# The second product of the attention logits, over 64 rows or over 128

## The chip, the cores and the metric

The kernel runs on one core of one Trainium2 chip. The metric is the device time of one execution in microseconds: 953.86 us, the median of three runs (953.65 to 954.18), before the change. Engine names in the profile: PE is the matrix engine (TensorE), PEld its weight loads, DVE the vector engine, ACT the scalar engine, POOL the GpSimd engine, SP the engine that issues most transfers.

## The reference, cut to what matters

One layer of a decoder trunk for 512 positions of width 1024: a norm and a modulation, one wide input projection, an mLSTM branch, a differential attention branch, gates and an output projection. The change touches the logits of the attention branch only. It has eight heads; each head has two maps of queries and keys of width 64, and the same bias for both:

```
logits = jnp.einsum('bhmqd,bhmkd->bhmqk', qh[:, :, :, q0:end], kh[:, :, :, :end])
p = jax.nn.softmax(logits + bias[None, :, None], axis=-1)
a = p[:, :, 0] - lam * p[:, :, 1]
```

`q0:end` is a block of 128 queries; its keys are all positions up to `end`, so a block has 128, 256, 384 or 512 keys.

## The kernel before, in words

**Arithmetic.** Matmuls read a 32-bit type that keeps fewer bits than float32. Every operand is therefore kept as a high part and a low part (what the high part left over), and a product is made of three matmuls: high by high, low by high, high by low (`mm3`, L135 to L137).

**Logits before.** A map is only 64 wide, and an operand tile has 128 partitions. `evac_qa` writes q of map 0 as a tile with the high part in partitions 0 to 63 (`LO`) and the low part in 64 to 127 (`HI`); for map 1 the halves are exchanged. `evac_ka` writes the high part of k of a map into both halves of a tile (`kh`), so that one matmul over all 128 rows (L441) gives high by high plus low by high. The third product, high q by low k, is a matmul of its own (L442). It takes only the 64 rows in which q has its high part: `q[m][a, qs]` with `kl[a, 0:wn]`. The low parts of k of both maps lie in one tile `kl`, map 0 in its lower half, map 1 in its upper half. For each head, four query blocks and two maps make eight such pairs of matmuls, with 256, 256, 384 and 512 columns in the four blocks (`wn`), so 64 pairs in all: 32 of 256 columns, 16 of 384, 16 of 512. The result of a pair lies in one of the four PSUM buffers tagged `core`, is read by DVE (L444, bias and row minimum) and then goes through an exponential on ACT (L446).

**Around it.** The attention heads are generators (`attn_head`) that are advanced by `tick()` between the projections (`proj_b`, `proj_v`), whose weights stream in as granules of 512 KB, are split by ACT (`whi`, L100) and DVE (`wlo`, L118), and are multiplied with the resident `h_hi` and `h_lo`. So short pieces of attention stand between long runs of projection matmuls. `inorder` fixes the order of the attention matmuls among themselves; otherwise each engine executes its instructions in the order in which a scheduler has put them when the program was built. The heads work from about 66 to 340 us. After the logits a head is transposed (L471, into `core` buffers), split into the tile `sw` (L100, L118), multiplied with v (L135 to L137 with `sw` and `v`) and normalised.

**Buffers.** Tiles of one tag share a ring of buffers; a tile's first write waits until the tile that had the buffer before has been read for the last time. `qk` has ten buffers: five for each head (two q, two `kh`, one `kl`), so two heads. The tag also serves the mLSTM's q and k and, at the end, `yh`. POOL has little to do: the masks of the bias tiles (L224), a zeroed strip in each `sw` (L464), and one-off fills (L509, L564).

Of the kernel before, what the change touches and what calls it, by code (L numbers as in the profile page):

```python
# [9 lines left out]
F32 = mybir.dt.float32  # L10
F32R = mybir.dt.float32r
AF = mybir.ActivationFunctionType
ALU = mybir.AluOpType

S = 512
D = 1024
P = 128
# [48 lines left out]
def hybrid_block_kernel(ctx: ExitStack, tc: tile.TileContext, xT, x, c, wada2, wada, win, wif, wpm, wpa, wout,  # L66
                        small, lamv, bif, relb, onehot, fing, out):
    nc = tc.nc
# [3 lines left out]
    sb = ctx.enter_context(tc.tile_pool(name="sb", bufs=1))  # L72
# [6 lines left out]
    def nm(s):  # L79
        _n[0] += 1  # L80
        return f"{s}_{_n[0]}"

    def tmp(w=512, dt=F32):
        return sb.tile([P, w], dt, tag="tmp", bufs=TB, name=nm("tmp"))

    def acc_ps():
        return acc.tile([P, 512], F32, tag="acc", name=nm("acc"))

    def core_ps():
        return core.tile([P, 512], F32, tag="core", name=nm("core"))  # L90

    def out_ps():
        return core.tile([P, 512], F32, tag="core", name=nm("core"))
# [32 lines left out]
    def inorder(inst):  # L126
        if last[0] is not None:
            tc.add_manual_dep(inst.ins, last[0].ins.name,
                              mybir.DependencyInfo(mybir.DependencyClass.NoSync, mybir.DependencyReason.DATA),
                              reason="issue order")  # L130
        last[0] = inst
# [40 lines left out]
    for k in range(NK):  # L172
        t = sb.tile([P, S], F32, tag="hp", bufs=16, name=nm("xt"))
# [10 lines left out]
    make_identity(nc, ident)  # L184
    onesf = const.tile([P, P], F32, name="onesf")
    nc.vector.memset(onesf, 1.0)
    ones_w = sb.tile([P, S], F32R, tag="qk", bufs=10, name="ones_w")
    nc.vector.memset(ones_w.bitcast(F32), 1.0)
    ones_r = const.tile([P, P], F32R, name="ones_r")
    nc.vector.tensor_copy(ones_r, onesf)  # L190
# [26 lines left out]
    def bias_tile(hd):  # L217
        if hd + 2 < AH:
            toe(hd + 2)
        bt = sb.tile([P, S], F32, tag="bt", bufs=3, name=nm("bt"))  # L220
        flat = toe_d[hd].rearrange("p l -> (p l)")
        v = flat[P - 1:P - 1 + P * (RL - 1)].rearrange("(p l) -> p l", l=RL - 1)[:, 0:S]
        nc.sync.dma_start(bt, v)
        a = nc.gpsimd.affine_select(bt[:, 384:512], bt[:, 384:512], [[-1, P]], ALU.is_ge, BIG, base=0,  # L224
                                    channel_multiplier=1)
        issue_after(a, x_done[0])
        return bt
# [17 lines left out]
    for i in range(2):  # L245
        ps = core_ps()
        a = nc.tensor.matmul(ps, onesf[0:1, :], crow[:, i * S:(i + 1) * S], start=True, stop=True)
# [19 lines left out]
    for k in range(NK):  # L267
        i, start = (0, k == 0) if k < 5 else (1, k == 5)
        sq = xsum[i] if start else tmp()
        a = nc.scalar.activation(sq, xt[k], AF.Square, scale=1.0 / 32)  # L270
# [36 lines left out]
    ps = core_ps()  # L307
# [21 lines left out]
    for (a, b) in ((0, 512), (512, RL)):  # L329
        ps = core_ps()  # L330
        m = nc.tensor.matmul(ps[0:AH, 0:b - a], relt, oneh[:, a:b], start=True, stop=True)  # L331
# [44 lines left out]
        return v  # L376

    def qk_tile():
        return sb.tile([P, S], F32R, tag="qk", bufs=10, name=nm("qk"))

    def silu2(ps):
        t = tmp()
# [8 lines left out]
    LO, HI = slice(0, 64), slice(64, 128)  # L391
# [9 lines left out]
        return q  # L401


    def evac_ka(ps):
        kh, kl = [], qk_tile()
        for a, b in ((LO, HI), (HI, LO)):
            t = qk_tile()
            nc.scalar.copy(t[a], ps[a])
            nc.scalar.copy(t[b], ps[a])
            nc.vector.tensor_tensor(kl[a], ps[a], t[a].bitcast(F32), ALU.subtract)  # L410
            kh.append(t)
        return kh, kl

    ha = [None] * AH
# [9 lines left out]
    def attn_head(hd, q, k):  # L424
        while live["p"] == PB:
            yield
        live["p"] += 1
        bt = bias_tile(hd)
        vs = slice((hd % 2) * P, (hd % 2) * P + P)
        pt = sb.tile([P, 2, 1280], F32, tag="p", bufs=PB, name=nm("pt"))  # L430
        mn = sb.tile([P, NT, 2], F32, tag="mn", bufs=3, name=nm("mn"))
        ls = sb.tile([P, NT, 2], F32, tag="ls", bufs=3, name=nm("ls"))
        kh, kl = k
        yield
        for qb in range(NT):
            w = P * (qb + 1)
            wn = max(w, 256)
            qs = slice(qb * P, qb * P + P)
            for m, a in enumerate((LO, HI)):
                ps = core_ps()[:, 0:wn]  # L440
                inorder(nc.tensor.matmul(ps, q[m][:, qs], kh[m][:, 0:wn], start=True, stop=False))  # L441
                inorder(nc.tensor.matmul(ps, q[m][a, qs], kl[a, 0:wn], start=False, stop=True))  # L442
                pp = pt[:, m, QOFF[qb]:QOFF[qb] + w]
                nc.vector.tensor_tensor_reduce(pp, ps[:, 0:w], bt[:, S - w:S], 1.0, BIG, ALU.add, ALU.min,  # L444
                                               mn[:, qb, m:m + 1])
                nc.scalar.activation(pp, pp, AF.Exp, scale=-1.0, bias=mn[:, qb, m:m + 1],  # L446
                                     accum_out=ls[:, qb, m:m + 1])
            if qb > 0:
                yield
        nc.vector.reciprocal(ls, ls)  # L450
        nc.vector.tensor_scalar(ls[:, :, 1], ls[:, :, 1], nlam, None, ALU.mult)
        for qb in range(NT):
            w = P * (qb + 1)
            p1 = pt[:, 0, QOFF[qb]:QOFF[qb] + w]
            p2 = pt[:, 1, QOFF[qb]:QOFF[qb] + w]
            nc.scalar.activation(p2, p2, AF.Copy, scale=ls[:, qb, 1:2])
            nc.vector.scalar_tensor_tensor(p1, p1, ls[:, qb, 0:1], p2, ALU.mult, ALU.add)
        yield
        while live["sw"]:
            yield  # L460
        live["sw"] = 1
        sw = sb.tile([P, 2, 1408], F32R, tag="sw", name=nm("sw"))
        ah, al = sw[:, 0, :], sw[:, 1, :]
        nc.gpsimd.memset(sw[:, :, 896:1024].bitcast(F32), 0.0)  # L464
        for kbs, o0 in (((0,), KOFF[0]), ((1,), KOFF[1]), ((3, 2), KOFF[3] + P)):
            ps = core_ps()
            n = 0
            for kb in kbs:
                for qb in range(kb, NT):
                    o = QOFF[qb] + kb * P  # L470
                    inorder(nc.tensor.transpose(ps[:, n:n + P], pt[:, 0, o:o + P], ident))  # L471
                    n += P
            split(ah[:, o0:o0 + n], al[:, o0:o0 + n], ps[:, 0:n])
        live["p"] -= 1
        yield
        ps = out_ps()
        for kb in range(NT):
            c0 = min(kb, 2) * P
            a = slice(KOFF[kb], KOFF[kb] + S - c0)
            mm3(ps[:, c0:S], (va[hd][0][:, kb, vs], va[hd][1][:, kb, vs]), (ah[:, a], al[:, a]),  # L480
                kb == 0, kb == NT - 1, head=True)
        live["sw"] = 0
        o_t = sb.tile([P, S], F32, tag="z", bufs=8, name=nm("o"))
        nc.scalar.copy(o_t, ps)
        sq = tmp()
        nc.scalar.activation(sq, ps, AF.Square)
        sh, sl = tmp(dt=F32R), tmp(dt=F32R)
        split(sh, sl, sq, eng="dve")
        yield
        ps = out_ps()  # L490
        inorder(nc.tensor.matmul(ps, ones_r, sh, start=True, stop=False))
        inorder(nc.tensor.matmul(ps, ones_r, sl, start=False, stop=True))  # L492
        r = rstd(ps, 1.0 / 128)
        nc.vector.tensor_mul(o_t, o_t, r)
        while za[hd] is None:
            yield
        z = za[hd]
        nc.vector.scalar_tensor_tensor(z, o_t, agc[:, hd:hd + 1], z, ALU.mult, ALU.mult)
        ha[hd] = hp_tiles()
        split(ha[hd][0], ha[hd][1], z, eng="dve")  # L500
# [83 lines left out]
    for k in range(NK):  # L584
# [5 lines left out]
        a = nc.scalar.copy(hi, raw)  # L590
        issue_after(a, recent["act"])
        recent["act"] = a
        t, b = xt[k], mod[:, k:k + 1]
# [32 lines left out]
        if k == 4:  # L626
# [9 lines left out]
            a = nc.vector.tensor_scalar(agc, sm[:, SM_AG:SM_AG + 8], -0.5 / 256 * (1.0 - LAM_INIT), None, ALU.mult)  # L636
            mgc = const.tile([P, 16], F32, name="mgc")
            issue_after(a, h_dve)
            a = nc.vector.tensor_scalar(mgc, sm[:, SM_MG:SM_MG + 16], -0.25 / 4096, None, ALU.mult)
# [31 lines left out]
    for p in range(1, 4):  # L671
        for i in range(2):
            hd = 2 * p + i
            q = evac_qa(proj_b(C_QA + 128 * hd))
# [18 lines left out]
    ps = core_ps()  # L693
# [178 lines left out]
    for h in range(MH):  # L872
        q, k, v, hv = [], [], [], []
# [28 lines left out]
        for d in range(4):  # L902
            ps = proj_b(C_OM + 512 * h + 128 * d)
            while len(hv) <= d:
                tick()
            t = tmp()
# [4 lines left out]
            else:  # L911
                t = tmp()
# [14 lines left out]
    for b in range(4, 8):  # L927
        ps = proj_b(C_GM + 128 * b, tick if b > 4 else None)
# [11 lines left out]
    def merge(b, ps):  # L940
        nc.vector.scalar_tensor_tensor(gt[b], gt[b], 1.0, ps, ALU.add, ALU.mult)
        nc.vector.tensor_add(gt[b], gt[b], ym[b])
        t = (sb.tile([P, S], F32R, tag="qk", bufs=10, name=nm("yh")),
             sb.tile([P, S], F32R, tag="hp", bufs=16, name=nm("yl")))
        split(t[0], t[1], gt[b], eng="act")
        yt.append(t)
# [26 lines left out]
    for t in range(NT):  # L973
# [5 lines left out]
        for n, ns in enumerate(parts):  # L979
            ps = first[n] if t == 0 else acc_ps() if n % 2 == 0 else core_ps()  # L980
            ps = ps[:, 0:ns.stop - ns.start]
# [83 lines left out]
```

## Time and profile before

| what | value |
|---|---|
| median of three runs | 953.86 us (953.65 to 954.18) |
| profiled execution, its own time | 953.58 us |
| its span in the trace | 951.6 us |
| what lies outside the span | 1.98 us |
| PE busy | 937.9 us (99%), 4735 matmuls |
| DVE busy | 603.7 us (63%) |
| ACT busy | 457.3 us (48%) |
| POOL busy | 17.1 us (2%) |

A row of the timeline gives the start, the duration, the engine, the source line, the operation, the tile written and those read, the shapes, and in brackets the idle time of the engine before it with what ended it. A matmul's end is modelled, and matmuls overlap: their durations say little, and what one costs is the distance from its start to the start of the next. For PE a shape such as `64*128 64x256` is 64 rows by 128 columns of weights, and 64 rows by 256 columns that move through them.

### The profile page before, as it was taken

The page shows a single profiled execution, that of the slowest core. Times are in us where ns is not written, and L with a number is a line of the kernel's source. Part 1 is how long each engine was busy: PE and PEld are TensorE (multiplying, and loading weights), DVE is VectorE, ACT ScalarE, POOL GpSimd, SP SyncE. Part 2 cuts the span into 40 slices and gives each one's busy share as a digit, 9 for nine tenths or more (in the row PEclk, how much of TensorE's full clock was granted, in tenths as well). Part 3 has the DMA queues.
Part 4 walks back from the last instruction along what each step waited for, and adds up shares of the span by engine and source line. Part 5 has one row for each costly group of instructions (what it writes and reads, how often), then busy time and mean ns, then how long its engine had stood idle before and what let it go on. Part 6 is the DMA issues. An engine that isn't in the chain of part 4 may idle for free.

```text
span 951.6 us, 12250 instructions
## 1 busy us (share of the span) xinstructions
PE 937.9 (99%) x4735; PEld 785.3 (83%) x4735; DVE 603.7 (63%) x975; ACT 457.3 (48%) x741; POOL 17.1 (2%) x40
## 2 busy tenths in 40 slices
PE   7999999999999999999999999999999999999997
PEld 3887877887788789888889888898888998888886
DVE  7966777866755637534658545486554776747954
ACT  7455777756556745312436433363223653226432
POOL 0000000000001000000000000000000000000000
PEclk8999999999999999999999999999999999999999
DMA  9872313433322253343222222222231224335421
GB/s 342 318 207 88 101 67 108 147 133 123 127 72 90 85 181 111 118 147 111 89 90 89 89 89 89 89 90 91 87 111 67 89 101 147 129 127 193 166 67 67
DMA packets 40659, 114.95 MB, mean 121 GB/s; under 512 B 8289, under 2 KB 8553, under 8 KB 39578
## 3 DMA queue, kind: packets, MB, share of 16 engines
q1 hardware_dynamic: 40010, 113.11, 34.3%
q10 hardware_dynamic: 592, 1.07, 0.3%
q8 instruction: 37, 0.61, 0.3%
q14 instruction: 20, 0.16, 0.1%
HBM read 106.78 MB, written 10.00 MB: 123 GB/s over the span
## 4 chain that ended last, share of the span: by engine, by line
PE 97%; DMA 1%; ACT 1%; DVE 1%; SPq 0%; issue 0%; ACTq 0%
PE acc L135 27%; PE acc L136 26%; PE acc L137 26%; PE core L135 4%; PE core L136 4%; PE core L137 4%; PE core L442 2%; PE core L441 2%; PE core L471 1%; DMA relt<-in_relb_dram 1%; PE core L238 1%; DMA xt<-in_xT_dram 1%; DVE wlo L118 0%; ACT whi L100 0%; PE core L331 0%; PE core L492 0%
## 5 line engine op out<-in xcount | busy, mean ns | idle before, releaser
L135 PE MATMUL acc<-h_hi,whi 128*128 128x512 f32 x688 | 271.0, 394 | 0.4 <-DVE qk L410 0.4
L118 DVE TENSOR_TENSOR wlo<-raw,whi 128x1024 fp32r<-128x1024 f32 x129 | 157.8, 1223 | 171.7 <-ACT whi L100 168.0
L100 ACT CAST whi<-raw 128x1024 fp32r<-128x1024 f32 x129 | 135.5, 1050 | 271.4 <-PE acc L136 217.4
L136 PE MATMUL acc<-h_lo,whi 128*128 128x512 f32 x656 | 256.5, 391 | 0.0
L137 PE MATMUL acc<-h_hi,wlo 128*128 128x512 f32 x656 | 255.7, 390 | 0.0
L135 PEld LDWEIGHTS acc<-h_hi,whi 128*128 128x128 f32 x688 | 129.4, 188 | 29.3 <-issue 1.5
L137 PEld LDWEIGHTS acc<-h_hi,wlo 128*128 128x128 f32 x656 | 123.2, 188 | 26.2
L136 PEld LDWEIGHTS acc<-h_lo,whi 128*128 128x128 f32 x656 | 123.3, 188 | 24.0 <-issue 0.4
L135 PE MATMUL acc<-whi,h_hi 128*128 128x256 f32 x352 | 100.1, 284 | 0.0
L137 PE MATMUL acc<-whi,h_lo 128*128 128x256 f32 x352 | 99.6, 283 | 0.0
L136 PE MATMUL acc<-wlo,h_hi 128*128 128x256 f32 x352 | 99.6, 283 | 0.0
L135 PE MATMUL acc<-hh,whi 128*128 128x512 f32 x192 | 74.8, 389 | 0.0
L136 PE MATMUL acc<-hl,whi 128*128 128x512 f32 x192 | 74.8, 389 | 0.0
L137 PE MATMUL acc<-hh,wlo 128*128 128x512 f32 x192 | 74.7, 389 | 0.0
L135 PEld LDWEIGHTS acc<-whi,h_hi 128*128 128x128 f32 x352 | 67.4, 191 | 1.7 <-issue 0.8
L136 PEld LDWEIGHTS acc<-wlo,h_hi 128*128 128x128 f32 x352 | 67.4, 192 | 0.6
L137 PEld LDWEIGHTS acc<-whi,h_lo 128*128 128x128 f32 x352 | 67.4, 192 | 0.0
L444 DVE CUSTOM_DVE_ANT_0 pt<-core,bt 128x128 f32<-128x128 f32 (+3 forms) x64 | 30.3, 487 | 29.7 <-PE core L442 29.5
L446 ACT ACTIVATE pt<-pt,mn 128x128 f32<-128x128 f32 (+3 forms) x64 | 35.6, 558 | 19.7 <-DVE mn L444 19.2
L137 PEld LDWEIGHTS acc<-hh,wlo 128*128 128x128 f32 x192 | 36.0, 188 | 7.5
L135 PEld LDWEIGHTS acc<-hh,whi 128*128 128x128 f32 x192 | 36.1, 188 | 7.3
L136 PEld LDWEIGHTS acc<-hl,whi 128*128 128x128 f32 x192 | 36.1, 188 | 7.2
(276 smaller groups left out, 1363.5 us busy)
## 6 DMA issues: line engine op xcount, KB each, us to landing
raw<-in_win_dram SPq DMA_DIRECT2D x112, 512.0 KB, 3.3
wa<-in_wada_dram SPq DMA_DIRECT2D x8, 1024.0 KB, 7.4
raw<-in_wpm_dram SPq DMA_DIRECT2D x16, 512.0 KB, 3.3
raw<-in_wada_dram SPq DMA_DIRECT2D x8, 512.0 KB, 3.4
raw<-in_wpa_dram SPq DMA_DIRECT2D x8, 512.0 KB, 3.3
raw<-in_wout_dram SPq DMA_DIRECT2D x8, 512.0 KB, 3.3
gt_d<-tmp SPq DMA_DIRECT2D x12, 256.0 KB, 2.2
toe_d<-rev_d SPq DMA_DIRECT2D x8, 320.0 KB, 7.0
```

What stands on the lines that cost most here:

```text
L100: recent["act"] = nc.scalar.copy(dst, src)
L118: recent["dve"] = nc.vector.tensor_tensor(lo, src, hi.bitcast(F32), ALU.subtract)
L135: a = nc.tensor.matmul(ps, lhs[0], rhs[0], start=start, stop=False)
L136: b = nc.tensor.matmul(ps, lhs[l[0]], rhs[l[1]], start=False, stop=False)
L137: c = nc.tensor.matmul(ps, lhs[r[0]], rhs[r[1]], start=False, stop=stop)
L238: a = nc.tensor.matmul(idle, ones_r, ones_w, start=True, stop=True)
L441: inorder(nc.tensor.matmul(ps, q[m][:, qs], kh[m][:, 0:wn], start=True, stop=False))
L442: inorder(nc.tensor.matmul(ps, q[m][a, qs], kl[a, 0:wn], start=False, stop=True))
L444: nc.vector.tensor_tensor_reduce(pp, ps[:, 0:w], bt[:, S - w:S], 1.0, BIG, ALU.add, ALU.min, mn[:, qb, m:m + 1])
L446: nc.scalar.activation(pp, pp, AF.Exp, scale=-1.0, bias=mn[:, qb, m:m + 1], accum_out=ls[:, qb, m:m + 1])
L471: inorder(nc.tensor.transpose(ps[:, n:n + P], pt[:, 0, o:o + P], ident))
```

## The change

The low part of k gets a tile for each map instead of half of a shared one. POOL fills the half of that tile in which q has its low part with zeros, and the second matmul takes all 128 rows: high q by low k in one half, low q by zero in the other, so its sum is the same. A head now has six `qk` tiles, and the ring grows from ten buffers to twelve. Their room comes from a scratch area for transfers that is reduced to 8192 (last hunk); no transfer of this kernel is issued by POOL, before or after.

```
     def evac_ka(ps):
-        kh, kl = [], qk_tile()
+        kh, kl = [], []
         for a, b in ((LO, HI), (HI, LO)):
-            t = qk_tile()
+            t, l = qk_tile(), qk_tile()
+            nc.gpsimd.memset(l[b].bitcast(F32), 0.0)
             nc.scalar.copy(t[a], ps[a])
             nc.scalar.copy(t[b], ps[a])
-            nc.vector.tensor_tensor(kl[a], ps[a], t[a].bitcast(F32), ALU.subtract)
+            nc.vector.tensor_tensor(l[a], ps[a], t[a].bitcast(F32), ALU.subtract)
             kh.append(t)
+            kl.append(l)
         return kh, kl
...
-            for m, a in enumerate((LO, HI)):
+            for m in range(2):
                 ps = core_ps()[:, 0:wn]
                 inorder(nc.tensor.matmul(ps, q[m][:, qs], kh[m][:, 0:wn], start=True, stop=False))
-                inorder(nc.tensor.matmul(ps, q[m][a, qs], kl[a, 0:wn], start=False, stop=True))
+                inorder(nc.tensor.matmul(ps, q[m][:, qs], kl[m][:, 0:wn], start=False, stop=True))
...
-        return sb.tile([P, S], F32R, tag="qk", bufs=10, name=nm("qk"))
+        return sb.tile([P, S], F32R, tag="qk", bufs=12, name=nm("qk"))
...
-    nc = _bacc.Bacc("TRN2", target_bir_lowering=False, num_devices=1)
+    nc = _bacc.Bacc("TRN2", target_bir_lowering=False, num_devices=1, dynamic_dma_scratch_size=8192)
```

The order of the instructions on PE, DVE, ACT and SP is as before. POOL gets 16 more. Its list between the bias masks of heads 3 and 4 (`bt_1308`, `bt_1647`) and that of head 5 (`bt_2052`), before:

```order
L224 AFFINE_SELECT bt_1308<-bt_1308 128x128
L224 AFFINE_SELECT bt_1647<-bt_1647 128x128
L464 MEMSET sw_1107 128x2x128
L464 MEMSET sw_1426 128x2x128
L564 MEMSET tmp_1278 4x512
L224 AFFINE_SELECT bt_2052<-bt_2052 128x128
```

The same place in the changed kernel (lines have moved by three), from the two new fills for head 2 (`qk_767`, `qk_773`) on:

```order
L409 MEMSET qk_767 64x512
L409 MEMSET qk_773 64x512
L224 AFFINE_SELECT bt_1320<-bt_1320 128x128
L224 AFFINE_SELECT bt_1662<-bt_1662 128x128
L467 MEMSET sw_1116 128x2x128
L467 MEMSET sw_1438 128x2x128
L409 MEMSET qk_1278 64x512
L567 MEMSET tmp_1290 4x512
L409 MEMSET qk_1284 64x512
L224 AFFINE_SELECT bt_2070<-bt_2070 128x128
```

The fills for head 3 (`qk_1278`, `qk_1284`) stand behind the fills of `sw` for heads 1 and 2 and around that of a `tmp` tile.

On PE, the first logits of head 3 before, with the engines that each waits for:

```order
L441 MATMUL core_1365<-qk_1269,qk_1179 128x256 [waits PE_49,Activation_49]
L442 MATMUL core_1365<-qk_1268,qk_1179 128x256 [waits DVE_49]
L441 MATMUL core_1370<-qk_1273,qk_1182 128x256 [waits DVE_49,Activation_49]
L442 MATMUL core_1370<-qk_1268,qk_1182 128x256 [waits DVE_49]
L441 MATMUL core_1375<-qk_1269,qk_1179 128x256
```

And in the changed kernel:

```order
L444 MATMUL core_1377<-qk_1277,qk_1188 128x256 [waits PE_49,Activation_49]
L445 MATMUL core_1377<-qk_1278,qk_1188 128x256 [waits DVE_49,Pool_49]
L444 MATMUL core_1382<-qk_1283,qk_1191 128x256 [waits DVE_49,Activation_49]
L445 MATMUL core_1382<-qk_1284,qk_1191 128x256 [waits DVE_49,Pool_49]
L444 MATMUL core_1387<-qk_1277,qk_1188 128x256
```

The rows stand in the same order; the first low product of each map now waits for POOL as well, and the two maps read different tiles (`qk_1278` and `qk_1284`) where both read `qk_1268`.

## Rows read from the trace of the kernel before

**Rows 1.** The page: PE's busy time, share and instructions; PE clock by slice.
```profile
PE 937.9 (99%) x4735; PEld 785.3 (83%) x4735; DVE 603.7 (63%) x975; ACT 457.3 (48%) x741; POOL 17.1 (2%) x40
PEclk8999999999999999999999999999999999999999
```
**Rows 2.** The page: the chain that ended last, shares by engine.
```profile
PE 97%; DMA 1%; ACT 1%; DVE 1%; SPq 0%; issue 0%; ACTq 0%
```
**Rows 3.** Windows: stretch, length, busy time and count of each engine, clock, DMA.
```profile
66.00:340.00 274.00, 273.47 (x1336) 217.64 (x1335) 186.39 (x395) 179.59 (x344) 8.21 (x18) 1.00 0.32 109
...
138.00:150.00 12.00, 12.00 (x48) 8.45 (x47) 11.69 (x20) 10.64 (x16) 0.91 (x1) 1.00 0.29 91
```
**Rows 4.** Waits of PE from 66 to 340: total, times, longest.
```profile
PE acc L135 <- DVE qk L410: 0.4, 1, 0.4
```
**Rows 5.** Timeline: start, duration; logits pairs of 256 columns, head 0.
```profile
76.62 0.38 PE L441 MATMUL core<-qk,qk 128*128 128x256 f32 x1
76.93 0.18 PEld L442 LDWEIGHTS core<-qk,qk 64*128 64x128 f32 x1
76.93 0.38 PE L442 MATMUL core<-qk,qk 64*128 64x256 f32 x1
77.24 0.38 PE L441 MATMUL core<-qk,qk 128*128 128x256 f32 x1
```
**Rows 6.** Timeline: pairs of 384 columns (head 0).
```profile
84.49 0.44 PE L441 MATMUL core<-qk,qk 128*128 128x384 f32 x1
...
85.23 0.44 PE L441 MATMUL core<-qk,qk 128*128 128x384 f32 x1
```
**Rows 7.** Timeline: a pair of 512 columns (head 3) and the matmuls behind it.
```profile
165.16 0.50 PE L441 MATMUL core<-qk,qk 128*128 128x512 f32 x1
...
166.01 0.50 PE L135 MATMUL acc<-h_hi,whi 128*128 128x512 f32 x1
166.35 0.40 PE L136 MATMUL acc<-h_lo,whi 128*128 128x512 f32 x1
```
**Rows 8.** Timeline: 128-row matmuls behind one another, of 256 and 384 columns.
```profile
36.38 0.28 PE L137 MATMUL core<-whi,h_lo 128*128 128x256 f32 x1
36.50 0.28 PE L135 MATMUL core<-whi,h_hi 128*128 128x256 f32 x1
...
184.77 0.33 PE L135 MATMUL core<-sw,v 128*128 128x384 f32 x1
184.94 0.34 PE L136 MATMUL core<-sw,v 128*128 128x384 f32 x1
```
**Rows 9.** Timeline: 128-row matmuls of 512 columns, with a weight load.
```profile
74.06 0.39 PE L135 MATMUL acc<-h_hi,whi 128*128 128x512 f32 x1
74.06 0.19 PEld L136 LDWEIGHTS acc<-h_lo,whi 128*128 128x128 f32 x1
74.29 0.39 PE L136 MATMUL acc<-h_lo,whi 128*128 128x512 f32 x1
```
**Rows 10.** Timeline of POOL: fills of 1024, 256 and 512 columns.
```profile
44.00 0.96 POOL L509 MEMSET wraw_if<- 128x1024 f32 x1 [2.06 <-DVE wlo L597]
...
131.53 0.31 POOL L464 MEMSET sw<- 128x256 f32 x1 [12.03 <-DVE qk L399]
135.54 0.74 POOL L564 MEMSET tmp<- 4x512 f32 x1 [3.70 <-DVE tmp L204]
```
**Rows 11.** Timeline: PE's first logits of head 3.
```profile
145.87 0.28 PE L441 MATMUL core<-qk,qk 128*128 128x256 f32 x1
```
**Rows 12.** Timeline, head 2: splits of head 1 on DVE, third logits pair.
```profile
121.94 1.61 DVE L118 TENSOR_TENSOR sw<-core,sw 128x512 fp32r<-128x512 f32 x3
...
123.28 0.28 PE L441 MATMUL core<-qk,qk 128*128 128x256 f32 x1
```
**Rows 13.** Timeline: DVE reads head 3's logits, then PE's transposes of head 2.
```profile
153.58 0.42 DVE L444 CUSTOM_DVE_ANT_0 pt<-core,bt 128x256 f32<-128x256 f32 x1
...
155.30 1.25 PE L471 MATMUL core<-ident,pt 128*128 128x128 f32 x10
```

More of the change, by code (lines that the diff above doesn't have):

```diff
@@ L186, in hybrid_block_kernel @@
     nc.vector.memset(onesf, 1.0)
-    ones_w = sb.tile([P, S], F32R, tag="qk", bufs=10, name="ones_w")
+    ones_w = sb.tile([P, S], F32R, tag="qk", bufs=12, name="ones_w")
     nc.vector.memset(ones_w.bitcast(F32), 1.0)
@@ L942, in merge @@
         nc.vector.tensor_add(gt[b], gt[b], ym[b])
-        t = (sb.tile([P, S], F32R, tag="qk", bufs=10, name=nm("yh")),
+        t = (sb.tile([P, S], F32R, tag="qk", bufs=12, name=nm("yh")),
              sb.tile([P, S], F32R, tag="hp", bufs=16, name=nm("yl")))
```

## The prediction

> **What bounds the kernel now.** I read the first part of the page first: the reader is to see that PE is busy for 99% of the span, DVE for 63%, and that the PE clock is full in every slice but the first [rows 1]. Then the chain that ended last: 97% of it is PE, so the time is the sum of what PE's instructions cost one behind another, and little else [rows 2]. Then the stretch in which the change acts, 66 to 340 us: PE has work in 273.5 of 274 us and waits once, for 0.4 us [rows 3, 4]. There a microsecond taken from PE is one taken from the kernel, as long as no other engine becomes late. DVE is busy for 186 of the 274 us, but unevenly: from 138 to 150 us it works for 11.7 of 12 us [rows 3].
>
> A busy PE does not tell what a matmul costs, so I then went to the timeline and read distances between starts.
>
> **What a pair costs now.** In a run of pairs of 256 columns the starts are at 76.62 (L441), 76.93 (L442) and 77.24 (the next L441): 0.62 us for a pair [rows 5]. For 384 columns a pair takes 85.23 - 84.49 = 0.74 us [rows 6], for 512 columns 166.01 - 165.16 = 0.85 us [rows 7].
>
> Plain 128-row matmuls behind one another stand closer: 36.50 - 36.38 = 0.12 us for 256 columns, 184.94 - 184.77 = 0.17 us for 384 [rows 8], 74.29 - 74.06 = 0.23 us for 512 [rows 9]. Two of them take 0.24, 0.34 and 0.46 us.
>
> The excess is 0.38, 0.40 and 0.39 us: the same at every width, so it isn't paid per column. It is twice the 0.18 us of a weight load [rows 5]. The rows also show why. Between 128-row matmuls the load of the next weights starts with the matmul before (both at 74.06), ahead of its own matmul at 74.29 [rows 9]; the 64-row load starts at 76.93 together with the matmul that needs it [rows 5], so it lies bare. This happens at each change of the number of rows, into L442 and out of it. A run of pairs pays the same in sum: its first L441 is followed 0.1 us sooner, but the first matmul behind the run is followed after 0.34 us (166.01 to 166.35) where 0.23 is plain [rows 7].
>
> **The change, part by part.**
>
> - *The second product over 128 rows.* PE keeps its number and order of matmuls. All now have 128 rows, so I take the plain distance for each. There are 32 pairs of 256 columns, 16 of 384 and 16 of 512: 32 x 0.38 + 16 x 0.40 + 16 x 0.39 = 12.2 + 6.4 + 6.2 = 24.8 us saved. Twice as many rows cost nothing in themselves: plain 128-row matmuls are what the distances above were taken from. The lower bound is no saving, if the loads stay bare; I take the upper value, the plain distance, since it is the same for projection weights and for the attention's own `sw` and `v` [rows 8, 9].
>
> - *Sixteen fills on POOL, half a tile of 512 columns each.* No row has this shape. The nearest are 0.31 us for 256 columns, 0.96 us for 1024, and 0.74 us for 512 columns of 4 partitions [rows 10]. Between 0.31 and 0.96 us each, I take 0.6: 10 us in all on an engine that is busy for 17 [rows 1]. What hides them is the time between a fill's turn and the logits that need it. POOL executes in order, and the fills of head 3 stand behind the `sw` fill of head 2 (131.53) and around the `tmp` fill, which waits for DVE until 135.54 [rows 10]. They would be done at about 137; PE's first logits of head 3 start at 145.87 [rows 11]. That leaves 9 us, and as these fills are released by DVE and PE, which move earlier along with the logits, most of it remains. I cost them at 0. Without that cover a head would pay its two fills, 8 x 2 x 0.6 = 10 us; with every fill at 0.96, 15 us.
>
> - *The waits on POOL.* Sixteen first low products wait for POOL as well. If they had to wait, the projection matmuls behind them on PE would be held back. By the margin above the fill is done long before, and the wait costs nothing.
>
> - *DVE's subtraction into the new tile* (L410) is the same work in another place.
>
> - *Twelve buffers.* Heads still reuse the buffers of the head before last, as before. The mLSTM's q and k may be written a little earlier, but the chain is PE's there too [rows 2]. 0 us.
>
> **What becomes late next.** DVE's and ACT's work between two pieces of attention stays as long as it is, while PE reaches the next piece sooner. At two places there is too little room. At head 2 the `core` buffers are given back by DVE's three splits of head 1, which take from 121.94 to 123.55, while the third pair starts at 123.28 [rows 12]; two pairs ahead of it become 0.77 us shorter, so I expect some 0.5 us of waiting. At head 3, DVE reads the last of four pairs until 154.00, and the transposes of head 2 start 1.3 us later, at 155.30 [rows 13]; PE would arrive there 4 x 0.38 = 1.5 us sooner, and two pairs of head 2 are saved before it too, in the stretch in which DVE has no room [rows 3]. I put this at 0.7 us. The later heads repeat the pattern with a little more room. Together I estimate 2.5 us, with 0 and 8 as bounds: 8 is half of what the pairs of the first five heads save, 5 x 8 x 0.39 = 15.6 us, for the case that DVE is full wherever it is now nearly so.
>
> **Sum.** 24.8 - 2.5 = 22.3 us. 953.58 - 22.3 = 931.3 us, against the profiled execution's own time, which stands 0.28 us under the median of the runs.
>
> **Rivals.**
>
> 1. *All of it arrives.* The waits above stay under 1 us, because the scheduler's order leaves enough projection matmuls between. For it: PE waits for 0.4 us in the whole stretch [rows 4]. Against: the two places just named. 953.6 - 24.4 = 929.2 us.
>
> 2. *DVE becomes the bound in the first five heads.* It gives back 8 us and more: 953.6 - 24.8 + 8 = 936.8 us. For it: 11.7 of 12 us busy [rows 3]. Against: over the stretch it has 88 us to spare [rows 3].
>
> 3. *The loads stay bare, and nothing changes.* Had the overlap been between loads and matmuls of different rows, each matmul would cost what L442 costs now, 0.31 us at 256 columns, and a pair 0.62 as before: 953.6 us. Against it stand the 128-row matmuls at 0.12 us behind one another [rows 8] and the load at 74.06 beside a matmul of the same 128 rows [rows 9].
>
> The Trainium skill states this rule: in "TensorE: Matmul & The Clock Gate", Part 3, weight loads overlap with running matmuls only where the row group differs. By it the 64-row form would be no worse than the full one, and the time would be that of this rival. The trace disagrees: the load at 74.06 runs beside a matmul of the same rows. The measurement decides, and I leave this rival a small chance only because no row shows two such loads of `qk` tiles in this stage.
>
> 4. *Slower: the zeros come late.* POOL's list is strictly in order, and a fill stands behind masks that wait for transfers and `sw` fills that wait for PE. If each fill of heads 2 to 7 came 15 us later than the rows let expect, beyond the margin of 9 us, PE would stand still for 6 us in each of the six heads: 953.6 - 22.3 + 36 = 967 us. It decides against the change from 9 + 22.3 / 6 = 12.7 us of delay on. For it: POOL's waits are long, 12 us before one fill [rows 10]. Against: nothing that releases these rows is moved back.
>
> **How the numbers follow.** Forecast 0.68, rival 1 0.15, rival 2 0.11, rival 3 0.03, rival 4 0.03. No change means within 0.2%, 1.9 us, which is about what a measurement of this kernel can tell. So faster 0.94, same 0.03, slower 0.03. The time is that of the forecast, 931.3 us. The range goes from 927.8, a little below rival 1 (a distance read to 0.01 us makes 1.3 us over 128 matmuls), to 937, where rival 2 is reached; rivals 3 and 4 and a heavier rival 2 are left out.
>
> **What would show it.** In the profile after: pairs of 256 columns at a distance of about 0.24 us, of 512 at 0.46; no weight load of 64 rows for `qk`; L135 behind a run of pairs followed after 0.23 us. Sixteen new fills on POOL of 0.3 to 1 us, each done some microseconds before its logits. PE's busy time about 22 us less, the waits of PE on DVE and ACT between 66 and 320 us grown to some 3 us, and nothing new after the attention. The forecast is wrong if the pairs stay above 0.5 us at 256 columns, if PE waits for POOL, or if waits for DVE exceed 8 us.

## The result, and the profile after

The changed kernel takes 929.97 us (median of four runs, 928.05 to 930.75) against 953.75 us before (952.13 to 954.18): a ratio of 0.9751, 95% interval 0.9736 to 0.9765. The forecast was 931.3 us, in a range from 927.8 to 937.0. The profiled execution took 929.48 us with a span of 927.3 us, 24.3 us less than before.

The first part of the page, as in [rows 1]: busy microseconds, share of the span, instructions.

```profile
PE 914.2 (99%) x4735; PEld 781.6 (84%) x4735; DVE 603.1 (65%) x975; ACT 455.0 (49%) x741; POOL 24.2 (3%) x56
```

PE executes as many matmuls as before and is busy for 23.7 us less; it still fills the span. DVE and ACT do the same work. POOL has 16 instructions more and 7 us more work.

The logits of head 0 on the timeline (start, duration), the place of [rows 5]. Lines have moved by three: L444 is the first product, L445 the second.

```profile
75.25 0.28 PE L444 MATMUL core<-qk,qk 128*128 128x256 f32 x1
75.36 0.28 PE L445 MATMUL core<-qk,qk 128*128 128x256 f32 x1
75.48 0.28 PE L444 MATMUL core<-qk,qk 128*128 128x256 f32 x1
75.60 0.28 PE L445 MATMUL core<-qk,qk 128*128 128x256 f32 x1
...
76.20 0.40 PE L135 MATMUL acc<-h_hi,whi 128*128 128x512 f32 x1
76.43 0.40 PE L136 MATMUL acc<-h_lo,whi 128*128 128x512 f32 x1
```

A pair of 256 columns takes 75.60 - 75.36 = 0.24 us where it took 0.62, and the matmul behind the run is followed after 0.23 us. A pair of 384 columns (82.55 to 82.90) and one of 512 (153.33 to 153.79), as in [rows 6, 7]:

```profile
82.55 0.34 PE L444 MATMUL core<-qk,qk 128*128 128x384 f32 x1
...
82.90 0.28 PE L444 MATMUL core<-qk,qk 128*128 128x256 f32 x1
...
153.33 0.39 PE L444 MATMUL core<-qk,qk 128*128 128x512 f32 x1
...
153.79 0.39 PE L135 MATMUL acc<-h_hi,whi 128*128 128x512 f32 x1
```

These are 0.35 and 0.46 us, where it was 0.74 and 0.85.

How much of this reaches the end is read from two landmarks: the first logits matmul of the kernel and the matmul behind the last. Of before:

```profile
76.10 0.28 PE L441 MATMUL core<-qk,qk 128*128 128x256 f32 x1
...
324.62 0.50 PE L135 MATMUL acc<-h_hi,whi 128*128 128x512 f32 x1
```

After, the first stands above at 75.25, and behind the last stands:

```profile
300.54 0.39 PE L135 MATMUL acc<-h_hi,whi 128*128 128x512 f32 x1
```

The stretch shrank from 248.52 to 225.29 us, by 23.2 us. From there to the end both traces take the same to 0.2 us. Another 0.85 us of the profiled difference lies ahead of the change: the first projection matmul starts at 21.13 us instead of 21.96. It isn't the change's doing: over the ten profiles of this study that start lies anywhere from 20.30 to 22.04 us, whatever the kernel. Single runs of one kernel differ by more, by 2.7 us for the changed kernel; how much of that lies in this start, no trace shows.

The waits of PE from 60 to 320 us (total, times, longest), as in [rows 4]:

```profile
PE acc L135 <- DVE qk L412: 0.5, 1, 0.5
PE core L474 <- DVE mn L447: 0.4, 1, 0.4
```

One wait is new: the transposes of head 2, one of the two places named. None is for POOL. Some shorter waits, which this view leaves out, follow further below. What POOL does around the logits of head 3, as in [rows 10], and then PE's first logits of that head, as in [rows 11]:

```profile
122.98 0.32 POOL L467 MEMSET sw<- 128x256 f32 x1 [10.47 <-PE core L137]
123.35 0.52 POOL L409 MEMSET qk<- 64x512 f32 x1
126.70 0.74 POOL L567 MEMSET tmp<- 4x512 f32 x1 [2.83 <-DVE tmp L204]
127.39 0.52 POOL L409 MEMSET qk<- 64x512 f32 x1
...
135.71 0.28 PE L444 MATMUL core<-qk,qk 128*128 128x256 f32 x1
```

The second fill ends at 127.91, 7.8 us before the logits; a fill takes 0.52 us.

### The profile page after: what moved, and what is told of

Same layout as the page of the kernel before. It is cut to its first block, busy times and chain, and to the rows that moved or that the text cites. A ratio compares the mean times of both kernels' runs of the same rounds, so it can differ in the third digit from the quotient of the medians.

```text
span 927.3 us, 12276 instructions
## 1 busy us (share of the span) xinstructions
PE 914.2 (99%) x4735; PEld 781.6 (84%) x4735; DVE 603.1 (65%) x975; ACT 455.0 (49%) x741; POOL 24.2 (3%) x56
## 4 chain that ended last, share of the span: by engine, by line
PE 94%; DVE 2%; DMA 2%; ACT 1%; issue 0%; SPq 0%; ACTq 0%; DVEq 0%
PE acc L135 26%; PE acc L136 26%; PE acc L137 26%; PE core L135 4%; PE core L136 4%; PE core L137 4%; PE core L444 1%; PE core L445 1%; PE core L474 1%; DMA relt<-in_relb_dram 1%; DVE wlo L118 1%; DMA xt<-in_xT_dram 1%; PE core L238 0%; ACT whi L100 0%; DMA raw<-in_win_dram 0%
## 5 line engine op out<-in xcount | busy, mean ns | idle before, releaser
L136 PEld LDWEIGHTS acc<-h_lo,whi 128*128 128x128 f32 x656 | 123.3, 188 | 23.7
```

The source lines that it names most:

```text
L136: b = nc.tensor.matmul(ps, lhs[l[0]], rhs[l[1]], start=False, stop=False)
```

## The experiments

The theory after the result: a change between 64 and 128 rows leaves a weight load bare, about 0.19 us each time, and the new form removes 128 such changes; nothing else in the change matters. The kernel before was measured again beside them: its median was 953.5 us beside the first four experiments and 953.98 us beside the other four.

**The buffers alone.** The kernel before, with twelve buffers and the smaller scratch (shown: the ring of the attention's tiles).

```
-        return sb.tile([P, S], F32R, tag="qk", bufs=10, name=nm("qk"))
+        return sb.tile([P, S], F32R, tag="qk", bufs=12, name=nm("qk"))
```

> The kernel before with twelve qk buffers and the smaller scratch, and nothing else. My theory (the gain is the row change on PE alone): no change, 953.8 us within 1. Rival (the two more buffers let work start earlier): a part of the 24 us shows here, 930 to 950 us.

Measured: 954.16 us, ratio 1.0011 (0.9995 to 1.0026). The buffers do nothing by themselves: in the trace the stretch between the two landmarks goes from 74.52 to 323.05 us, 248.5 us as before. Two of its ten runs took 957.49 and 958.44 us, for which no trace shows a reason; the other eight lie between 951.96 and 954.47.

**The rows alone.** No fills, ten buffers; the second product reads `kh` over all rows.

```
-                inorder(nc.tensor.matmul(ps, q[m][a, qs], kl[a, 0:wn], start=False, stop=True))
+                inorder(nc.tensor.matmul(ps, q[m][:, qs], kh[m][:, 0:wn], start=False, stop=True))
```

> The kernel before with ten buffers, no fills, and a second product over all 128 rows that reads kh again in place of the low part of k (so the low part is left out of the logits). My theory: the row change alone gives all, 930 us within 1.5, as the changed kernel. Rival (the sixteen fills or the waits on POOL cost something in the changed kernel): faster than the changed kernel by up to 10 us, 920 to 928. Rival (the buffers are needed): 940 or more.

Measured: 929.52 us, ratio 0.9749 (0.9734 to 0.9763), as the changed kernel. So the row change gives the whole gain, and the fills, the waits on POOL and the new tiles cost nothing that can be seen.

**Half of the pairs.** The changed kernel, with 128 rows for map 0 only.

```
+                ar = slice(0, P) if m == 0 else HI
-                inorder(nc.tensor.matmul(ps, q[m][:, qs], kl[m][:, 0:wn], start=False, stop=True))
+                inorder(nc.tensor.matmul(ps, q[m][ar, qs], kl[m][ar, 0:wn], start=False, stop=True))
```

> The changed kernel, but only map 0 takes 128 rows in its second product; map 1 takes the 64 rows as before. My theory (0.19 us for each change of the number of rows, two for each pair): half the changes are gone, 64 x 0.19 = 12 us saved, 941.8 us within 1.5. Rival (the cost was that both maps read one kl tile): all of the gain stays, 930 us.

Measured: 941.88 us, ratio 0.9877 (0.9861 to 0.9894): half of the gain, though each map has its own `kl` tile here. Sharing the tile was not the cost. Both forms stand side by side in its timeline (first products L444, second L446, weight loads as PEld):

```profile
74.52 0.28 PE L444 MATMUL core<-qk,qk 128*128 128x256 f32 x1
74.53 0.19 PEld L446 LDWEIGHTS core<-qk,qk 128*128 128x128 f32 x1
74.64 0.28 PE L446 MATMUL core<-qk,qk 128*128 128x256 f32 x1
74.75 0.28 PE L444 MATMUL core<-qk,qk 128*128 128x256 f32 x1
74.96 0.18 PEld L446 LDWEIGHTS core<-qk,qk 64*128 64x128 f32 x1
74.96 0.38 PE L446 MATMUL core<-qk,qk 64*128 64x256 f32 x1
75.27 0.19 PEld L444 LDWEIGHTS core<-qk,qk 128*128 128x128 f32 x1
75.28 0.39 PE L444 MATMUL core<-qk,qk 128*128 128x256 f32 x1
```

The load of 128 rows starts at 74.53, beside the matmul of 74.52, and its own matmul follows at 74.64. The load of 64 rows starts only at 74.96, 0.21 us after the matmul of 74.75 and at the same time as its own matmul; the next load of 128 rows, at 75.27, likewise.

**The maps grouped.** 64 rows as before, but both first products, then both second products.

```
-            for m, a in enumerate((LO, HI)):
-                ps = core_ps()[:, 0:wn]
-                inorder(nc.tensor.matmul(ps, q[m][:, qs], kh[m][:, 0:wn], start=True, stop=False))
-                inorder(nc.tensor.matmul(ps, q[m][a, qs], kl[a, 0:wn], start=False, stop=True))
+            pss = [core_ps()[:, 0:wn] for _ in range(2)]
+            for m in range(2):
+                inorder(nc.tensor.matmul(pss[m], q[m][:, qs], kh[m][:, 0:wn], start=True, stop=False))
+            for m, a in enumerate((LO, HI)):
+                inorder(nc.tensor.matmul(pss[m], q[m][a, qs], kl[a, 0:wn], start=False, stop=True))
+            for m in range(2):
+                ps = pss[m]
```

> The kernel before, 64 rows, but the two maps are grouped: both first products, then both second products, the lower rows and then the upper rows. Theory A (a change of the number of rows costs 0.19 us; from lower to upper half is free): half the changes are gone, 12 us saved, 942 us. Theory B (each load of 64 rows lies bare, and the first load behind one): three of four loads still bare, 6 us saved, 948 us. Theory C (as A, and the two halves run at the same time): 12 + 32 x 0.16 = 17 us saved, 937 us.

Measured: 935.52 us, ratio 0.9813 (0.9798 to 0.9828), 18 us saved: nearest to theory C, by which it was 17. In the trace the stretch between the two landmarks goes from 74.65 to 306.32 us and is 16.9 us shorter than before. Its timeline, where two instructions of one line are merged into a row (x2); L443 is the second product:

```profile
75.30 0.50 PE L441 MATMUL core<-qk,qk 128*128 128x256 f32 x2
75.73 0.19 PEld L443 LDWEIGHTS core<-qk,qk 64*128 64x128 f32 x2
75.73 0.38 PE L443 MATMUL core<-qk,qk 64*128 64x256 f32 x2
76.04 0.19 PEld L135 LDWEIGHTS acc<-h_hi,whi 128*128 128x128 f32 x1
76.04 0.50 PE L135 MATMUL acc<-h_hi,whi 128*128 128x512 f32 x1
```

From the start of the two 64-row matmuls to the next load it is 76.04 - 75.73 = 0.31 us, as for a single one before (0.31 us, [rows 5]): both run at once, and so do their loads. Two pairs take 76.04 - 75.30 = 0.74 us. That is three plain distances, since the second products share one, and two changes of rows: 3 x 0.12 + 2 x 0.19. The new form takes 4 x 0.12 = 0.48 and stays ahead: to run the halves at once saves one distance for two pairs, and the two changes of rows cost more than that at every width here (0.23 at most against 0.38).

**All matmuls over 64 rows**, map 0 below, map 1 above.

```
-                inorder(nc.tensor.matmul(ps, q[m][:, qs], kh[m][:, 0:wn], start=True, stop=False))
+                inorder(nc.tensor.matmul(ps, q[m][a, qs], kh[m][a, 0:wn], start=True, stop=False))
```

> The kernel before with both products over 64 rows: map 0 on the lower rows, map 1 on the upper (the low part of q is left out of the logits). Theory (the cost is the change between 64 and 128 rows, and the two halves can run at once): changes are left only at the ends of the 27 runs of pairs, 27 x 2 x 0.19 = 10 us of the 25; and where an upper matmul follows a lower one they overlap, 5 to 8 us more: 931 to 934 us. Rival (a load of 64 rows lies bare whatever stands before it): 128 bare loads, 953 us or more.

Measured: 934.63 us, ratio 0.98 (0.9784 to 0.9817), just outside what the theory gave, 931 to 934 us. The rival is out: 128 matmuls of 64 rows cost less than 64 did before. The first run of pairs:

```profile
76.23 0.39 PE L441 MATMUL core<-qk,qk 64*128 64x256 f32 x2
76.46 0.28 PE L442 MATMUL core<-qk,qk 64*128 64x256 f32 x2
76.58 0.28 PE L441 MATMUL core<-qk,qk 64*128 64x256 f32 x2
76.69 0.28 PE L442 MATMUL core<-qk,qk 64*128 64x256 f32 x2
76.91 0.50 PE L135 MATMUL acc<-h_hi,whi 128*128 128x512 f32 x1
```

Two pairs take 76.58 - 76.23 = 0.35 us with the bare load of the run's beginning, and 0.23 us without it (76.46 to 76.69). PE is so quick here that it waits for DVE to give `core` buffers back; one of its waits from 66 to 330 us:

```profile
PE core L441 <- DVE mn L444: 0.8, 4, 0.4
```

**All matmuls over the lower 64 rows**, so that neither the number of rows nor the half changes inside a run.

```
-                inorder(nc.tensor.matmul(ps, q[m][:, qs], kh[m][:, 0:wn], start=True, stop=False))
-                inorder(nc.tensor.matmul(ps, q[m][a, qs], kl[a, 0:wn], start=False, stop=True))
+                inorder(nc.tensor.matmul(ps, q[m][LO, qs], kh[m][LO, 0:wn], start=True, stop=False))
+                inorder(nc.tensor.matmul(ps, q[m][LO, qs], kl[LO, 0:wn], start=False, stop=True))
```

> The kernel before with both products of both maps over the lower 64 rows (the upper rows, that is the low part of q and the right k of map 1, are left out). No half ever changes, so nothing can run beside anything. Theory (a load of the same rows is hidden behind the running matmul): only the ends of the 27 runs cost, 25 - 10 = 15 us saved, 939 us within 2. Rival (loads overlap only with matmuls of other rows): every pair costs as before or more, 953 us or above.

Measured: 940.14 us, ratio 0.985 (0.9834 to 0.9866): the theory's 939. The timeline at the beginning of a run:

```profile
75.79 0.39 PE L137 MATMUL acc<-h_hi,wlo 128*128 128x512 f32 x1
76.10 0.18 PEld L441 LDWEIGHTS core<-qk,qk 64*128 64x128 f32 x1 [0.35 <-issue]
76.11 0.38 PE L441 MATMUL core<-qk,qk 64*128 64x256 f32 x1
76.21 0.19 PEld L442 LDWEIGHTS core<-qk,qk 64*128 64x128 f32 x1
76.33 0.28 PE L442 MATMUL core<-qk,qk 64*128 64x256 f32 x1
76.33 0.18 PEld L441 LDWEIGHTS core<-qk,qk 64*128 64x128 f32 x1
76.44 0.28 PE L441 MATMUL core<-qk,qk 64*128 64x256 f32 x1
```

Only the first load of 64 rows is bare: it starts 0.31 us after the matmul before. A later one starts 0.11 us ahead of its own matmul (76.33 against 76.44), and the matmuls there stand 0.11 us apart, as those of 128 rows do. So it is not the 64 rows that cost, but the change.

The rows also split what a change costs. The matmul of 75.79 has 512 columns, and the next could start 0.23 us later; the bare load starts 0.31 us later, so 0.08 us go by before it begins. The matmul of 76.11 is followed after 76.33 - 76.11 = 0.22 us, where 0.11 is plain: another 0.11 us, for the load that nothing hides. The 0.19 us are thus about half a load that lies bare and half a pause ahead of that load; what PE does in the pause no row shows.

**Four times the fills.** Each fill is made four times on POOL.

```
+            for _ in range(4):
-            nc.gpsimd.memset(l[b].bitcast(F32), 0.0)
+                nc.gpsimd.memset(l[b].bitcast(F32), 0.0)
```

> The changed kernel with each of POOL's sixteen fills made four times, 25 us more on POOL, in the same place of its list. Theory (the fills lie in POOL's idle time, 7 us and more ahead of the logits): no change, 930 us within 1.5. Rival (the fills disturb DVE, or PE waits for them): slower by a good part of 25 us, 940 us or more.

Measured: 930.06 us, ratio 0.9751 (0.9736 to 0.9765), as with single fills. POOL's group of fills in its profile:

```profile
L410 POOL MEMSET qk<- 64x512 f32 x64 | 33.8, 529 | 19.9 <-PE core L446 16.5
```

34 us of fills are hidden as 8 us were.

**The fills on DVE.**

```
-            nc.gpsimd.memset(l[b].bitcast(F32), 0.0)
+            nc.vector.memset(l[b].bitcast(F32), 0.0)
```

> The changed kernel with the sixteen fills on DVE instead of POOL. Theory (DVE has room in the attention stretch but for two places): 0 to 2 us slower than the changed kernel, 930 to 932 us. Rival (DVE is at its limit in the first five heads, so each fill of some 0.3 to 0.5 us there is paid): 4 us and more slower, 934 us or above.

Measured: 929.84 us, ratio 0.9747 (0.9733 to 0.9762). DVE carries sixteen fills more, 0.49 us each, and it costs nothing that the median shows; the rival falls. The trace shows how near that is: from the first projection matmul to the matmul behind the last logits it takes 279.8 us (21.94 to 301.74), the changed kernel 279.4 (21.13 to 300.54). PE's instructions don't quite stand in the same order here (the first product of logits starts at 69.91, 48.0 us behind the first projection matmul, where it was 54.1), so the 0.4 us are not the price of the fills alone.

No version beats the changed kernel beyond the intervals; the three with more, other or no fills equal it.

## Why the prediction was right

- *The cost of a pair and its cause.* 0.62, 0.74 and 0.85 us became 0.24, 0.35 and 0.46, as worked out from [rows 8, 9] (0.34 for the middle one). That the excess belongs to the change of rows and not to the columns, the shared tile or the 64 rows themselves is shown by three results together: half the changes gone give half the gain (941.88 us), 64-row matmuls behind one another stand as close as 128-row ones, and the load of 64 rows is bare only where the matmul before has 128. One reading was too simple: the excess of 0.38 us is not two whole loads of 0.18 us that lie bare. That the figures agree is luck; a change costs about half of its 0.19 us before its load begins, as the kernel with all matmuls over the lower rows shows. The sum doesn't rest on it, since it was made from distances between starts.

- *The sum.* 24.8 us was expected from the pairs and 2.5 us back for waits; the stretch shrank by 23.2. So about 1.6 us came back, and the term for the waits was 0.9 us too large. At head 3 the forecast of 0.7 us holds. The transposes of head 2 come 11.01 us earlier (155.30 to 144.29, [rows 13]), and two projection matmuls shortly ahead of them 11.72 and 11.53 (149.99 to 138.27 and 154.27 to 142.74): 0.2 us are lost between those two and 0.5 behind them. The second wait stands in the row of the transposes:

```profile
144.16 0.42 DVE L447 CUSTOM_DVE_ANT_0 pt<-core,bt 128x256 f32<-128x256 f32 x1
144.29 1.31 PE L474 MATMUL core<-ident,pt 128*128 128x128 f32 x10 [0.36 <-DVE mn L447]
```

- Most of the rest lies in heads 4 to 7, where the prediction named no place. A run of four pairs there loses time at its fourth pair, too little at a time to stand in the view of waits. Head 4:

```profile
174.11 0.29 DVE L447 CUSTOM_DVE_ANT_0 pt<-core,bt 128x128 f32<-128x128 f32 x1
...
174.27 0.28 PE L445 MATMUL core<-qk,qk 128*128 128x256 f32 x1
174.46 0.39 PE L444 MATMUL core<-qk,qk 128*128 128x256 f32 x1
174.68 0.28 PE L445 MATMUL core<-qk,qk 128*128 128x256 f32 x1
```

  The starts are 0.19 and 0.22 us apart where 0.12 is plain, so 0.17 us are lost; with the same at 214.51, 247.60 and 287.66 it makes 0.7 us. The fourth pair starts 0.06 us after DVE has read the first one (174.11 + 0.29 = 174.40), so I take it that it waits for that pair's `core` buffer; no run tests this.

- At head 2, 0.5 us was expected at the third pair and nothing came:

```profile
114.66 1.61 DVE L118 TENSOR_TENSOR sw<-core,sw 128x512 fp32r<-128x512 f32 x3
...
115.26 0.40 PE L135 MATMUL acc<-h_hi,whi 128*128 128x512 f32 x1
115.40 0.19 PEld L444 LDWEIGHTS core<-qk,qk 128*128 128x128 f32 x1 [0.18 <-DVE sw L118]
115.49 0.29 PE L444 MATMUL core<-qk,qk 128*128 128x256 f32 x1
```

  The load of its weights waited 0.18 us for a split, but the matmul starts 115.49 - 115.26 = 0.23 us after the one before, the plain distance of 512 columns. The third pair moved from 123.28 to 115.49, by 7.79 us, the splits from 121.94 to 114.66, by 7.28 [rows 12]. I had let DVE stand still while PE moved; but ahead of the splits DVE was itself waiting for what PE delivers, so it moved up with it. In the kernel before:

```profile
121.12 0.29 DVE L444 CUSTOM_DVE_ANT_0 pt<-core,bt 128x128 f32<-128x128 f32 x1 [0.42 <-PE core L442]
```

- *Nothing on POOL.* Right: no wait of PE for POOL, and four times the work made no difference. A fill takes 0.52 us, within the bounds of 0.31 and 0.96, near the 0.6 taken. The margin at head 3 was 7.8 us instead of 9.

- *Twelve buffers at nothing.* Right, by the run with the buffers alone.

- *The rivals.* Rival 1 (waits under 1 us, 929.2 us) lies closer to the median than the forecast does; with 1.6 us given back the truth stands between the two, and the interval of the ratio, some 1.4 us to either side, doesn't tell them apart. Rival 2 falls: 1.6 us came back where it asks for 8, and DVE had room for sixteen fills more. Rival 3, the one that the Trainium skill's rule gives ("TensorE: Matmul & The Clock Gate", Part 3: loads overlap only with matmuls of another row group), falls twice: loads of 128 rows start beside matmuls of 128 rows (74.53 beside 74.52, with map 0 over 128 rows), and loads of the lower 64 rows start ahead of their own matmul, while matmuls of the same rows run (76.33 against 76.44). Rival 4 did not come.

## What to carry to other kernels

On a kernel that PE bounds, read the distance between starts of neighbouring matmuls, not their durations or the busy share: an excess that is the same at every width is not paid per column; here it was paid at each change of the number of rows, 0.19 us in each direction. Where short products of 64 rows stand among those of 128, pad them with zeros, as long as an engine with idle time writes the zeros well ahead. Before pricing the waits that a faster engine would meet, ask whether the other engine was itself waiting for it; if so it moves up too.

## What was not expected

Matmuls on the lower and on the upper 64 rows that stand behind one another run at the same time: 0.31 us for two of 256 columns in the grouped kernel, where one takes 0.31. In the kernel with all matmuls over 64 rows the code issues two products of map 0 and then two of map 1, yet the trace shows the first products of both maps together (76.23) and then the second ones (76.46): the upper half's first product doesn't wait for the lower half's second, which the code issues ahead of it. Two pairs then take 0.23 us instead of 0.48. It doesn't pay here, since a change of rows at both ends of each of 27 short runs costs more; in a long run of 64-row products it would weigh more, which no run here shows.
